# A decoder layer's MLP: a third seven-product unit in one column half, its weight sums made in the up stage, and the order of the returns and of the end

## The chip, the cores and the metric

The kernel runs on one core of one Trainium2 chip. Time is device microseconds (us) of that core, the median of several runs. The profile is one execution taken by the hardware profiler.

## The reference, cut to what matters

One decoder layer: a gated mix of sparse attention and retention, cross-attention, then an MLP, for 256 tokens of width 2048 in float32. The change touches only the MLP and the final norm (lines 1032 on). The MLP's hidden width is 8192.

```python
nm = rmsnorm(h, mlp_norm_w)
h = h + jnp.square(jax.nn.relu(nm @ w_up)) @ w_down
...
return rmsnorm(h, final_norm_w)
```

## The kernel before

**Engines.** PE (TensorE) multiplies, DVE (VectorE) and ACT (ScalarE) work on whole tiles, POOL (GpSimd) makes a power, SP starts loads. Each float32 operand is split into a high part of type fp32r (ACT copies it, L162) and a low part, the rest (DVE subtracts, L163). A product is then three matmuls: high x high, high x low, low x high. In the up stage the moving operand carries high and low tokens side by side: a high weight block takes one matmul of 512 columns, a low one a matmul of 256 (L158 is the helper that records every matmul).

**Pieces and units.** `mlp` cuts the hidden width into four pieces `p` of 2048 columns. A piece has an *up stage* of 16 units `Up(j, c)`: column block `j` (512 hidden columns, four PSUM banks), quarter `c` of the width 2048; 32 matmuls each. Below, up unit (3,0) is the first unit of the last block. Then comes a *down stage* of two halves `c` of the output columns (1024 each) with eight units `n` (256 hidden rows each). A *plain* unit (kind P, L1185) makes 8 products, 24 matmuls of 512 columns. A *seven-product* unit (kind S, L1170) makes 7 products, 21 matmuls, by Strassen and Winograd's scheme; it needs sums of weight blocks (`t1`, `t2`, made in `Down.prep`, L1134) and of activation blocks (`sums_up`, L1108). The string `KINDS` says which `n` are of kind S: 2 and 4 of eight, in both halves.

**PSUM.** Eight banks. Blocks `j` 0 and 2 use the two double tiles of pool `mm`, blocks 1 and 3 the other four banks. In a half, the double tiles `xa` (first 128 tokens) and `xb` (last 128) collect the plain products; the other four banks collect what is special to kind S (`m`). After the last S unit of a half, `combine` (L1197) makes two rows of sums from those banks, and `fold` (L1207) adds them to the result `hres`. `evac` (L1212) adds `xa` and `xb` to `hres` at the half's end. The next up stage begins in the double tiles that `evac` frees.

**Order.** The loop at the end of `mlp` (L1270 on) writes the order out: for each unit first the *next* unit's `prep` (load, high parts, low parts), then this unit's matmuls, then the `posts` that are due. A block's posts are `add_up` (adds the banks, right behind the block's last unit), `square_up` (relu, square, split; one unit later) and `sums_up` (two units later). Instructions go through `pin` (L153), which keeps each behind what was written before it on its own engine: DVE, ACT and SP run in that order. Loads take one of three `raw` buffers, high and low parts one of four buffers each.

**The end.** The last two units of the last piece are run as one pair (`plain` with two units): for each row block `i`, for each column half `j`, for each unit. `evac` then takes 1024 columns, `finish` (L1234) squares them on ACT (`scale`, L1225), multiplies with the final norm's weights on DVE, gets the power from POOL, scales four tiles of 512 columns (two on DVE, two on ACT) and starts the output transfers. `plain` also returns `scale` as a post at the end of each half of the last piece.

Of the kernel before, what the change touches and what calls it, by code (L numbers as in the profile page):

```python
# [9 lines left out]
F32 = mybir.dt.float32  # L10
F32R = mybir.dt.float32r
AF = mybir.ActivationFunctionType
ALU = mybir.AluOpType
# [4 lines left out]
P = 128  # L18
T = 256
D = 2048  # L20
EPS = 1e-6
# [44 lines left out]
class Kern:  # L66
# [86 lines left out]
    def pin(self, ins):  # L153
        if self.ordered:
            self.tc.keep_in_program_order(ins)
# [876 lines left out]
    def mlp(self):  # L1032
        nc, a = self.nc, self.a
        V, A, G, PE = nc.vector, nc.scalar, nc.gpsimd, nc.tensor
        pin = self.pin
        NP, KINDS = 4, "PPSPSPPP"
        hres = {}
        s8, r2 = self.keep("hs8", [2, 4]), self.keep("r2", [2])
        f8, ft = self.keep("fs", [2, 2]), self.keep("ft", [2])
        fw = []  # L1040
        tt = lambda o, x, y, op: pin(V.tensor_tensor(o, x, y, op=op))
        act = lambda o, x, f=AF.Copy, **kw: pin(A.activation(o, x, f, **kw))
# [7 lines left out]
        def hilo(n=1024):  # L1050
            return (self.st.tile([P, 1024], F32R, name=self.nm("hi"), tag="hi")[:, :n],
                    self.st.tile([P, 1024], F32R, name=self.nm("lo"), tag="lo")[:, :n])
# [12 lines left out]
        class Up:  # L1065
# [12 lines left out]

            def body(u):
                o = u.piece["banks"] = u.banks() if u.c == 0 else u.piece["banks"]  # L1080
                for k in range(4):
                    kt = u.c * 4 + k
                    x = self.h2hl[kt // 2][:, kt % 2, :]
                    for b in range(4):
                        s = slice(b * P, (b + 1) * P)
                        h, l = u.w[k]
                        self.mul(o[b], h[:, s], x, kt == 0, False)
                        self.mul(o[b][:, 0:T], l[:, s], x[:, 0:T], False, kt == 15)
                    if (u.p, u.j) == (0, 0) and k % 2 == 1:
                        back(u.c, k // 2)  # L1090
                return [self.add_up, self.square_up, self.sums_up] if u.c == 3 else []

        def add_up(u):
# [14 lines left out]
        def sums_up(u):  # L1108
            for k in range(2):
                n = 2 * u.j + k  # L1110
                if KINDS[n] != "S":
                    continue
                v = u.y[:, 2 * k:2 * k + 2, :].rearrange("p k (i t) -> p k i t", i=2)
                a11, a21, a12, a22 = v[:, 0, 0, :], v[:, 0, 1, :], v[:, 1, 0, :], v[:, 1, 1, :]
                s, sh, sl = self.w2("ss"), self.w2("sh", 512, F32R), self.w2("sl", 512, F32R)
                s1, s2, s3, s4 = (s[:, q * P:(q + 1) * P] for q in range(4))
                tt(s1, a21, a22, ALU.add)
                tt(s2, s1, a11, ALU.subtract)
                tt(s3, a21, a11, ALU.subtract)
                tt(s4, a12, s2, ALU.subtract)  # L1120
                self.split(sh, sl, s)
                u.piece["sums"][n] = [(sh[:, q * P:(q + 1) * P], sl[:, q * P:(q + 1) * P]) for q in range(4)]
# [5 lines left out]
        class Down:  # L1128
            def __init__(u, p, c, n, piece, group):
                u.p, u.c, u.n, u.piece, u.g = p, c, n, piece, group  # L1130
                u.kind = KINDS[n]
                u.last_s = n == max(k for k in range(8) if KINDS[k] == "S")

            def prep(u):  # L1134
                r0, c0 = u.p * 2048 + u.n * 256, u.c * 1024
                raw = load(a["w_down"][0][r0:r0 + 256, c0:c0 + 1024], 2)
                if u.kind == "P":
                    u.w = halves(raw)
                    return
                q = raw.rearrange("p (q n) -> p q n", q=4)  # L1140
                t1, t2 = self.big("t1", F32, (2, 512)), self.big("t2", F32, (2, 512))
                tt(t1, q[:, 1:2, :].to_broadcast([P, 2, 512]), q[:, 0::3, :], ALU.subtract)
                bh, bl = hilo()
                dh, dl = hilo(512)
                self.split(bh, bl, raw[:, 1024:])
                tt(t2[:, 0, :], q[:, 3, :], t1[:, 0, :], ALU.subtract)
                tt(t2[:, 1, :], q[:, 2, :], t2[:, 0, :], ALU.subtract)
                self.split(dh, dl, q[:, 0, :])
                (h1, l1), (h2, l2) = [[self.big(n, F32R, (2, 512)) for n in ("th", "tl")] for _ in range(2)]
                self.split(h1, l1, t1)  # L1150
                self.split(h2, l2, t2)
                u.w = {1: (dh, dl), 2: (bh[:, :512], bl[:, :512]), 3: (bh[:, 512:], bl[:, 512:]),
                       5: (h1[:, 0, :], l1[:, 0, :]), 7: (h1[:, 1, :], l1[:, 1, :]),
                       6: (h2[:, 0, :], l2[:, 0, :]), 4: (h2[:, 1, :], l2[:, 1, :])}

            def product(u, m, x, w, last):
                (xh, xl), (h, l) = x, w
# [12 lines left out]
            def body(u):  # L1170
                bank = u.g["bank"]
                if not bank:
                    ab, cd = u.g["rows"] = self.mmt("xa"), self.mmt("xb")
                    bank.update({2: ab[:, :512], 3: ab[:, 512:], 4: cd[:, :512], 8: cd[:, 512:]})
                if u.kind == "P":
                    return u.plain([u])
                if 1 not in bank:
                    bank.update({1: self.pst("m1"), 6: self.pst("m6"), 7: self.pst("m7"), 5: self.pot("m5")})
                s1, s2, s3, s4 = u.piece["sums"][u.n]
                x = {1: u.x(0, 0), 2: u.x(1, 0), 3: s4, 4: u.x(1, 1), 5: s1, 6: s2, 7: s3}  # L1180
                for m in (2, 3, 1, 5, 7, 6, 4):
                    u.product(m, x[m], u.w[m], u.last_s and m in (1, 5, 6, 7))
                return [combine, fold] if u.last_s else []

            def plain(u, us):  # L1185
                end = us[-1].n == 7
                for i in range(2):
                    for j in range(2):
                        for v in us:
                            for k in range(2):  # L1190
                                v.product((2, 3, 4, 8)[2 * i + j], v.x(k, i), v.w[2 * k + j], end and v is us[-1] and k == 1)
                    if end:
                        evac(us[-1], i)
                return [lambda u: scale(u.c)] if end and u.p == NP - 1 else []


        def combine(u):  # L1197
# [11 lines left out]
                o = hres[i, u.c]  # L1209
                stt(o, u.g["xy"][i], r2[:, i:i + 1], o, ALU.mult, ALU.add)  # L1210

        def evac(u, i):  # L1212
            o, c = hres[i, u.c], u.c
            stt(o, u.g["rows"][i], r2[:, i:i + 1], o, ALU.mult, ALU.add)
            if u.p < NP - 1:
                return
            if not fw:
                for k in range(2):
                    fw.append(self.big("fw", F32, (1024,)))
                    nc.scalar.dma_start(fw[k], a["final_norm_w"][k * 1024:(k + 1) * 1024].partition_broadcast(P))  # L1220
            if c == 1:
                finish(i)


        def scale(c, rows=range(2)):  # L1225
            for i in rows:
                o, v = hres[i, c], ft[:, i:i + 1]
                junk = self.big("junk", F32, (1024,))
                act(junk, o, AF.Square, accum_out=f8[:, i, c:c + 1])
                tt(o, o, fw[c], ALU.mult)  # L1230
                if c == 0:
                    pin(V.tensor_scalar(v, f8[:, i, 0:1], 1.0 / D, EPS, op0=ALU.mult, op1=ALU.add))

        def finish(i):  # L1234
            scale(1, [i])
            v = ft[:, i:i + 1]
            stt(v, f8[:, i, 1:2], 1.0 / D, v, ALU.mult, ALU.add)
            G.tensor_tensor(v, v, self.mhalf, op=ALU.pow)
            for k in range(4):
                o = hres[i, k // 2][:, (k % 2) * 512:(k % 2) * 512 + 512]  # L1240
                if k % 2:
                    act(o, o, scale=v)
                else:
                    pin(V.tensor_scalar(o, o, v, None, op0=ALU.mult))
                (nc.scalar if k % 2 else nc.sync).dma_start(self.out[0, i * P:(i + 1) * P, k * 512:(k + 1) * 512], o)
# [27 lines left out]
        while n < len(units):  # L1273
            u = units[n]
            two = n == len(units) - 2
            if n + 1 < len(units):
                units[n + 1].prep()
            self.ordered = True
            late = u.plain([u, units[n + 1]]) if two else u.body()
            posts += [[k, u, f] for k, f in enumerate(late)]  # L1280
            for t in list(posts):
                if t[0] == 0:
                    posts.remove(t)
                    t[2](t[1])
                else:
                    t[0] -= 1
            n += 2 if two else 1
# [29 lines left out]
```

## Time and profile before

| what | us |
|---|---|
| median of 3 runs | 1943.82 (1943.37 to 1943.91) |
| the profiled execution, its own time | 1943.98 |
| its span in the profile | 1942.2 |
| PE busy | 1916.1 (99%) |
| DVE busy | 1288.1 (66%) |
| ACT busy | 969.5 (50%) |

The span runs from the first to the last recorded event; the execution's own time is 1.8 us longer. Matmuls are pipelined and their ends are modelled, so what one costs PE in a stream is read as the distance from one start to the next. Idle time of an engine is put down to what released it.

### The profile page before, as it was taken

How to read it: one execution, taken by the hardware profiler on the slowest of the kernel's cores; microseconds unless marked ns; L12 is line 12 of the kernel's file. 1: busy time of each engine (PE TensorE's matmuls, PEld its weight loads, DVE VectorE, ACT ScalarE, POOL GpSimd, SP SyncE). 2: the span in 40 equal slices, each digit the busy share in tenths (PEclk: the TensorE clock that was granted, in tenths of full speed). 3: DMA queues.
4: the chain of work that ended last, by engine and by line, in shares of the span. 5: the costliest groups of instructions: out<-in, count | busy, mean ns of one | idle time of the engine just before them, and what ended most of it. 6: DMA issues, size and time to landing. Idle time of an engine off the chain costs nothing.

```text
span 1942.2 us, 26311 instructions
## 1 busy us (share of the span) xinstructions
PE 1916.1 (99%) x10534; PEld 1652.9 (85%) x10534; DVE 1288.1 (66%) x1553; ACT 969.5 (50%) x1308; POOL 85.4 (4%) x101
## 2 busy tenths in 40 slices
PE   8999999999999999999999999999999999999997
PEld 6888889888889999888889999888888888888885
DVE  6554577655766656887556756668757866875687
ACT  6444444455555554776444546544445434543554
POOL 1100021000000000321000000000000000000000
PEclk9999999999999999999999999999999999999999
DMA  8655545777877775333566654555655655665653
GB/s 267 211 177 195 182 168 171 238 239 247 282 242 242 251 247 193 130 125 114 195 220 220 211 176 151 165 189 188 195 182 186 211 180 178 198 201 185 193 195 130
DMA packets 173771, 382.17 MB, mean 197 GB/s; under 512 B 10592, under 2 KB 18784, under 8 KB 173648
## 3 DMA queue, kind: packets, MB, share of 16 engines
q1 hardware_dynamic: 169344, 373.96, 57.8%
q10 hardware_dynamic: 3504, 4.20, 0.7%
q0 software_dynamic: 800, 2.33, 0.4%
q8 instruction: 82, 1.34, 0.3%
q14 instruction: 41, 0.34, 0.1%
HBM read 374.17 MB, written 6.29 MB: 196 GB/s over the span
## 4 chain that ended last, share of the span: by engine, by line
PE 96%; DVE 2%; DMA 1%; issue 0%; ACT 0%; POOLq 0%; POOL 0%; SPq 0%; ACTq 0%; DVEq 0%
PE x L158 35%; PE u L158 18%; PE w L158 18%; PE xa L158 8%; PE xb L158 7%; PE acc L158 3%; PE m L158 2%; PE o L158 1%; PE s L158 1%; PE ro L158 1%; PE pT L816 1%; DVE lo L163 1%; DMA anw<-in_attn_norm_w_dram 0%; PE tr L287 0%; DVE hres L1043 0%
## 5 line engine op out<-in xcount | busy, mean ns | idle before, releaser
L163 DVE TENSOR_TENSOR lo<-raw,hi 128x1024 fp32r<-128x1024 f32 (+1 forms) x688 | 831.9, 1227 | 455.3 <-ACT hi L162 440.6
L162 ACT ACTIVATE hi<-raw 128x1024 fp32r<-128x1024 f32 (+1 forms) x688 | 704.6, 1047 | 688.1 <-PE x L158 336.2
L158 PE MATMUL u<-nhl,hi 128*128 128x512 f32 x1024 | 362.5, 398 | 3.5 <-DVE hres L1043 2.0
L158 PE MATMUL u<-nhl,lo 128*128 128x256 f32 x1024 | 288.0, 281 | 0.0
L158 PE MATMUL x<-hi,xh 128*128 128x512 f32 x704 | 283.0, 402 | 2.3 <-ACT hi L162 2.3
L158 PE MATMUL x<-hi,xl 128*128 128x512 f32 x704 | 278.3, 395 | 0.0
L158 PE MATMUL x<-lo,xh 128*128 128x512 f32 x704 | 277.5, 394 | 0.0
L158 PEld LDWEIGHTS u<-nhl,hi 128*128 128x128 f32 x1024 | 192.3, 188 | 50.9 <-DVE hres L1043 3.0
L158 PEld LDWEIGHTS u<-nhl,lo 128*128 128x128 f32 x1024 | 193.1, 189 | 0.1
L158 PEld LDWEIGHTS x<-lo,xh 128*128 128x128 f32 x704 | 133.2, 189 | 30.9 <-DVE lo L163 0.8
L158 PEld LDWEIGHTS x<-hi,xh 128*128 128x128 f32 x704 | 133.0, 189 | 30.3 <-ACT hi L162 2.7
L158 PEld LDWEIGHTS x<-hi,xl 128*128 128x128 f32 x704 | 133.1, 189 | 26.6
L158 PE MATMUL w<-xh,hi 128*128 128x256 f32 x512 | 145.2, 284 | 0.0
L158 PE MATMUL w<-xh,lo 128*128 128x256 f32 x512 | 144.2, 282 | 0.0
L158 PE MATMUL w<-xl,hi 128*128 128x256 f32 x512 | 144.1, 281 | 0.0
L158 PEld LDWEIGHTS w<-xh,hi 128*128 128x128 f32 x512 | 96.8, 189 | 1.4
L158 PEld LDWEIGHTS w<-xl,hi 128*128 128x128 f32 x512 | 96.8, 189 | 1.4
L158 PEld LDWEIGHTS w<-xh,lo 128*128 128x128 f32 x512 | 96.8, 189 | 0.0
L158 PE MATMUL w<-mh,hi 128*128 128x256 f32 x320 | 90.6, 283 | 0.0
L158 PE MATMUL w<-ml,hi 128*128 128x256 f32 x320 | 90.0, 281 | 0.0
L158 PE MATMUL w<-mh,lo 128*128 128x256 f32 x320 | 90.0, 281 | 0.0
L158 PE MATMUL xa<-lo,hh 128*128 128x512 f32 x208 | 81.8, 393 | 0.6 <-DVE lo L163 0.6
(310 smaller groups left out, 3016.6 us busy)
## 6 DMA issues: line engine op xcount, KB each, us to landing
raw<-in_w_in_dram SPq DMA_DIRECT2D x119, 1024.0 KB, 4.9
raw<-in_w_up_dram SPq DMA_DIRECT2D x64, 1024.0 KB, 5.4
raw<-in_w_down_dram SPq DMA_DIRECT2D x64, 1024.0 KB, 5.4
raw<-in_cmp_w_k_dram SPq DMA_DIRECT2D x16, 1024.0 KB, 4.9
raw<-in_w_b_dram SPq DMA_DIRECT2D x16, 1024.0 KB, 5.4
raw<-in_cmp_w_v_dram SPq DMA_DIRECT2D x16, 1024.0 KB, 5.0
raw<-in_w_a_dram SPq DMA_DIRECT2D x16, 1024.0 KB, 5.1
raw<-in_w_out_dram SPq DMA_DIRECT2D x16, 1024.0 KB, 5.1
```

The source lines that it names most:

```text
L158: self.pin(self.nc.tensor.matmul(out, l, r, start=start, stop=stop, skip_group_check=True))
L162: self.pin(self.nc.scalar.activation(hi, src, AF.Copy))
L163: self.pin(self.nc.vector.tensor_tensor(lo, src, hi.bitcast(F32), op=ALU.subtract))
L816: PE.transpose(pt[:, r * P:(r + 1) * P], sms[r // 2][:, r % 2, c:c + P], self.ident)
```

## The change

Half 0 of the output columns now takes kind S at `n` 1, 3 and 5, half 1 at 3 and 5. A block's activation sums are made if either half needs them. The weight sums of a down stage's first S unit are made behind up unit (3,0) (`ahead`), from a load of their own; the unit itself then only splits the blocks that enter as they are. The first up unit of pieces 1 to 3 does all four of its contraction steps for the first two banks, then for the other two. In the last pair the first row block goes unit by unit, the second column half by column half, and each half of 512 columns is evacuated, squared and multiplied by itself; in the last half `combine` and `fold` both stand right behind the last S unit. The final norm's weights are loaded where the first half is scaled, no longer where it is evacuated, and the second half is no longer scaled once more by a post. Three of the four last scalings run on DVE.

```diff
-        NP, KINDS = 4, "PPSPSPPP"
+        NP, KINDS = 4, ("PSPSPSPP", "PPPSPSPP")
...
@@ Up.body
+                late = u.p > 0 and (u.j, u.c) == (0, 0)
+                for bs in ((0, 1), (2, 3)) if late else (range(4),):
+                    for k in range(4):
...
+                        for b in bs:
...
@@ sums_up
-                if KINDS[n] != "S":
+                if "S" not in (KINDS[0][n], KINDS[1][n]):
...
@@ Down.prep
+                sums = None if u.early else u.sums(raw)
+                if sums:
+                    next(sums)
+                bh, bl = hilo()
+                dh, dl = hilo(512)
+                self.split(bh, bl, raw[:, 1024:])
+                if sums:
+                    next(sums)
+                self.split(dh, dl, raw[:, :512])
+                if sums:
+                    next(sums)
...
+            def sums(u, raw):
                 q = raw.rearrange("p (q n) -> p q n", q=4)
                 t1, t2 = self.big("t1", F32, (2, 512)), self.big("t2", F32, (2, 512))
                 tt(t1, q[:, 1:2, :].to_broadcast([P, 2, 512]), q[:, 0::3, :], ALU.subtract)
+                yield
                 tt(t2[:, 0, :], q[:, 3, :], t1[:, 0, :], ALU.subtract)
                 tt(t2[:, 1, :], q[:, 2, :], t2[:, 0, :], ALU.subtract)
+                yield
+                u.early = []
+                for t in (t1, t2):
+                    u.early.append([self.big(n, F32R, (2, 512)) for n in ("th", "tl")])
+                    self.split(*u.early[-1], t)
+                yield
+
+            def ahead(u):
+                r0, c0 = u.p * 2048 + u.n * 256, u.c * 1024
+                for _ in u.sums(load(a["w_down"][0][r0:r0 + 256, c0:c0 + 1024], 2)):
+                    pass
...
@@ Down.body
-                return [combine, fold] if u.last_s else []
+                return [lambda u: (combine(u), fold(u))] if (u.p, u.c) == (NP - 1, 1) else [combine, fold]
...
@@ plain
+                    order = [(v, j) for v in us for j in range(2)] if i == 0 else [(v, j) for j in range(2) for v in us]
+                    for v, j in order:
+                        for k in range(2):
+                            v.product((2, 3, 4, 8)[2 * i + j], v.x(k, i), v.w[2 * k + j], end and v is us[-1] and k == 1)
+                        if end and len(us) == 2 and v is us[-1]:
+                            evac(u, i, j)
+                    if end and len(us) == 1:
+                        evac(u, i)
+                return [scale] if end and u.p == NP - 1 and u.c == 0 else []
...
+        def evac(u, i, j=None):
+            c, p = u.c, u.p
+            v = slice(0, 1024) if j is None else slice(j * 512, j * 512 + 512)
+            o = hres[i, c][:, v]
+            stt(o, u.g["rows"][i][:, v], r2[:, i:i + 1], o, ALU.mult, ALU.add)
+            if j is not None:
+                square(i, c, v, 1 + j)
+                if j == 1:
+                    finish(i)
+
+        def square(i, c, v, n):
+            o = hres[i, c][:, v]
+            junk = self.big("junk", F32, (1024,))[:, v]
+            act(junk, o, AF.Square, accum_out=f8[:, i, n:n + 1])
+            tt(o, o, fw[c][:, v], ALU.mult)
+
+        def scale(u):
+            for k in range(2):
+                fw.append(self.big("fw", F32, (1024,)))
+                pin(nc.scalar.dma_start(fw[k], a["final_norm_w"][k * 1024:(k + 1) * 1024].partition_broadcast(P)))
+            for i in range(2):
+                square(i, 0, slice(0, 1024), 0)
+                pin(V.tensor_scalar(ft[:, i:i + 1], f8[:, i, 0:1], 1.0 / D, EPS, op0=ALU.mult, op1=ALU.add))
 
         def finish(i):
-            scale(1, [i])
             v = ft[:, i:i + 1]
-            stt(v, f8[:, i, 1:2], 1.0 / D, v, ALU.mult, ALU.add)
+            for n in (1, 2):
+                stt(v, f8[:, i, n:n + 1], 1.0 / D, v, ALU.mult, ALU.add)
...
-                if k % 2:
+                if k == 1:
                     act(o, o, scale=v)
...
@@ the loop
             posts += [[k, u, f] for k, f in enumerate(late)]
+            if isinstance(u, Up) and (u.j, u.c) == (3, 0):
+                next(d for d in units[n:] if isinstance(d, Down) and d.kind == "S").ahead()
```

## Rows read from the trace of the kernel before

**Rows 1.** Busy time by stretch, last piece: stretch, length, then PE to POOL, clock, DMA.
```profile
1752.30:1843.50 91.20, 90.51 (x514) 78.58 (x513) 54.74 (x63) 40.79 (x52) 0.00 (x0) 1.00 0.58 187
1843.50:1930.30 86.80, 86.15 (x372) 69.57 (x371) 72.67 (x78) 42.72 (x50) 0.55 (x1) 1.00 0.48 162
```
**Rows 2.** The chain that ended last: start, length, what; twelve matmuls of 512 columns.
```profile
1912.63 2.77 PE xa L158 x12
```
**Rows 3.** PE in order of time at piece 1's start: start, duration, instruction, [idle].
```profile
1398.66 0.28 PE L158 MATMUL u<-nhl,lo 128*128 128x256 f32 x1
1399.61 0.51 PE L158 MATMUL u<-nhl,hi 128*128 128x512 f32 x1 [0.68 <-DVE hres L1043]
```
**Rows 4.** DVE in order of time, last piece, up units (3,0) and (3,1).
```profile
1823.71 2.36 DVE L163 TENSOR_TENSOR lo<-raw,hi 128x1024 fp32r<-128x1024 f32 x2 [0.52 <-ACT hi L162]
1825.99 1.22 DVE L1043 SCALAR_TENSOR_TENSOR relu<-relu 128x1024 f32<-128x1024 f32 x1
...
1829.48 2.35 DVE L163 TENSOR_TENSOR lo<-raw,hi 128x1024 fp32r<-128x1024 f32 x2
```
**Rows 5.** ACT in order of time, the same units.
```profile
1827.24 1.06 ACT L162 ACTIVATE hh<-relu 128x1024 fp32r<-128x1024 f32 x1 [2.62 <-DVE relu L1043]
1828.20 2.00 ACT L162 ACTIVATE hi<-raw 128x1024 fp32r<-128x1024 f32 x2
```
**Rows 6.** PE in order of time, last piece, start of up unit (3,2).
```profile
1832.24 0.28 PE L158 MATMUL u<-nhl,lo 128*128 128x256 f32 x1
```
**Rows 7.** DVE in order of time: weights of a seven-product unit, last piece.
```profile
1850.65 1.22 DVE L1041 TENSOR_TENSOR t<-raw 128x1024 f32<-128x1024 f32 x1
1851.78 1.22 DVE L163 TENSOR_TENSOR lo<-raw,hi 128x1024 fp32r<-128x1024 f32 x1
1852.92 1.42 DVE L1041 TENSOR_TENSOR t<-raw,t 128x512 f32<-128x512 f32 x2
...
1854.85 2.35 DVE L163 TENSOR_TENSOR tl<-t,th 128x1024 fp32r<-128x1024 f32 x2
```
**Rows 8.** PE in order of time, last units: behind kind S, in the pair, last.
```profile
1912.47 0.39 PE L158 MATMUL xa<-hi,hh 128*128 128x512 f32 x1
...
1920.52 0.50 PE L158 MATMUL xa<-lo,hh 128*128 128x512 f32 x1 [0.48 <-DVE lo L163]
...
1930.08 0.39 PE L158 MATMUL xb<-lo,hh 128*128 128x512 f32 x1
```
**Rows 9.** DVE in order of time, last units and the end.
```profile
1912.05 0.69 DVE L1041 TENSOR_TENSOR u<-m,ux 128x512 f32<-128x512 f32 x1 [1.63 <-PE m L158]
...
1930.51 1.28 DVE L1043 SCALAR_TENSOR_TENSOR hres<-xb,r,hres 128x1024 f32<-128x1024 f32 x1 [0.20 <-PE xb L158]
1933.01 1.23 DVE L1041 TENSOR_TENSOR hres<-hres,fw 128x1024 f32<-128x1024 f32 x1 [1.22 <-ACT junk L1042]
...
1934.97 0.88 DVE L1244 TENSOR_SCALAR hres<-hres,ft 128x512 f32<-128x512 f32 x2 [0.67 <-POOL ft L1238]
...
1940.02 1.23 DVE L1041 TENSOR_TENSOR hres<-hres,fw 128x1024 f32<-128x1024 f32 x1 [0.36 <-DMA out_dram<-hres]
```
**Rows 10.** Groups by shape, ACT squares of 512 columns: busy us, mean ns, idle before.
```profile
L1042 ACT ACTIVATE junk<-hr 128x512 f32<-128x512 f32 x8 | 4.8, 599 | 14.0 <-DVE hres L1255 14.0
```
**Rows 11.** The chain that ended last: the last output transfer.
```profile
1936.87 3.03 DMA out_dram<-hres
```
**Rows 12.** The tile of the final norm's weights: transfers from issue to landing.
```profile
DMA to landing us min/median/max: 4.2/5.0/5.9
```
**Rows 13.** DVE in order of time, last piece: first use of those weights.
```profile
1887.62 1.22 DVE L1041 TENSOR_TENSOR hres<-hres,fw 128x1024 f32<-128x1024 f32 x1
```
**Rows 14.** PE in order of time at the kernel's start.
```profile
12.76 0.63 PE L158 MATMUL x<-hi,xl 128*128 128x512 f32 x1
13.19 0.63 PE L158 MATMUL x<-lo,xh 128*128 128x512 f32 x1
```
**Rows 15.** Busy time by stretch behind the last matmul; the clock is third from the end.
```profile
1935.00:1936.00 1.00, 0.00 (x0) 0.00 (x0) 0.86 (x2) 0.70 (x1) 0.00 (x0) 0.63 0.00 0
```

More of the change, by code (lines that the diff above doesn't have):

```diff
@@ L1035, in mlp @@
         pin = self.pin
-        NP, KINDS = 4, "PPSPSPPP"
+        NP, KINDS = 4, ("PSPSPSPP", "PPPSPSPP")
         hres = {}
         s8, r2 = self.keep("hs8", [2, 4]), self.keep("r2", [2])
-        f8, ft = self.keep("fs", [2, 2]), self.keep("ft", [2])
+        f8, ft = self.keep("fs", [2, 3]), self.keep("ft", [2])
         fw = []
@@ L1080, in body @@
                 o = u.piece["banks"] = u.banks() if u.c == 0 else u.piece["banks"]
[L1081 to L1090, printed above, removed]
+                late = u.p > 0 and (u.j, u.c) == (0, 0)
+                for bs in ((0, 1), (2, 3)) if late else (range(4),):
+                    for k in range(4):
+                        kt = u.c * 4 + k
+                        x = self.h2hl[kt // 2][:, kt % 2, :]
+                        for b in bs:
+                            s = slice(b * P, (b + 1) * P)
+                            h, l = u.w[k]
+                            self.mul(o[b], h[:, s], x, kt == 0, False)
+                            self.mul(o[b][:, 0:T], l[:, s], x[:, 0:T], False, kt == 15)
+                        if (u.p, u.j) == (0, 0) and k % 2 == 1:
+                            back(u.c, k // 2)
                 return [self.add_up, self.square_up, self.sums_up] if u.c == 3 else []
@@ L1114, in sums_up @@
                 a11, a21, a12, a22 = v[:, 0, 0, :], v[:, 0, 1, :], v[:, 1, 0, :], v[:, 1, 1, :]
-                s, sh, sl = self.w2("ss"), self.w2("sh", 512, F32R), self.w2("sl", 512, F32R)
+                s = self.w2("ss")
+                if len(u.piece["sums"]) < 2:
+                    sh, sl = self.w2("sh", 512, F32R), self.w2("sl", 512, F32R)
+                else:
+                    both = self.big("sb", F32R, (2, 512))
+                    sh, sl = both[:, 0, :], both[:, 1, :]
                 s1, s2, s3, s4 = (s[:, q * P:(q + 1) * P] for q in range(4))
@@ L1130, in __init__ @@
                 u.p, u.c, u.n, u.piece, u.g = p, c, n, piece, group
-                u.kind = KINDS[n]
-                u.last_s = n == max(k for k in range(8) if KINDS[k] == "S")
+                u.kind = KINDS[c][n]
+                u.last_s = n == KINDS[c].rindex("S")
+                u.early = None
             def prep(u):
@@ L1139, in prep @@
                     return
+                sums = None if u.early else u.sums(raw)
[9 more added lines that the diff above has]
+                    next(sums)
+                (h1, l1), (h2, l2) = u.early
+                u.w = {1: (dh, dl), 2: (bh[:, :512], bl[:, :512]), 3: (bh[:, 512:], bl[:, 512:]),
+                       5: (h1[:, 0, :], l1[:, 0, :]), 7: (h1[:, 1, :], l1[:, 1, :]),
+                       6: (h2[:, 0, :], l2[:, 0, :]), 4: (h2[:, 1, :], l2[:, 1, :])}
+            def sums(u, raw):
                 q = raw.rearrange("p (q n) -> p q n", q=4)
@@ L1142, in prep @@
                 tt(t1, q[:, 1:2, :].to_broadcast([P, 2, 512]), q[:, 0::3, :], ALU.subtract)
-                bh, bl = hilo()
-                dh, dl = hilo(512)
-                self.split(bh, bl, raw[:, 1024:])
+                yield
                 tt(t2[:, 0, :], q[:, 3, :], t1[:, 0, :], ALU.subtract)
                 tt(t2[:, 1, :], q[:, 2, :], t2[:, 0, :], ALU.subtract)
[L1148 to L1154, printed above, removed]
+                yield
[8 more added lines that the diff above has]
+                    pass
             def product(u, m, x, w, last):
@@ L1182, in body @@
                     u.product(m, x[m], u.w[m], u.last_s and m in (1, 5, 6, 7))
-                return [combine, fold] if u.last_s else []
+                if not u.last_s:
+                    return []
+                return [lambda u: (combine(u), fold(u))] if (u.p, u.c) == (NP - 1, 1) else [combine, fold]
             def plain(u, us):
@@ L1187, in plain @@
                 for i in range(2):
[L1188 to L1194, printed above, removed]
+                    order = [(v, j) for v in us for j in range(2)] if i == 0 else [(v, j) for j in range(2) for v in us]
[7 more added lines that the diff above has]
+                return [scale] if end and u.p == NP - 1 and u.c == 0 else []
         def combine(u):
@@ L1210, in fold @@
                 stt(o, u.g["xy"][i], r2[:, i:i + 1], o, ALU.mult, ALU.add)
[L1212 to L1232, printed above, removed]
+        def evac(u, i, j=None):
[19 more added lines that the diff above has]
+                pin(V.tensor_scalar(ft[:, i:i + 1], f8[:, i, 0:1], 1.0 / D, EPS, op0=ALU.mult, op1=ALU.add))
         def finish(i):
-            scale(1, [i])
             v = ft[:, i:i + 1]
-            stt(v, f8[:, i, 1:2], 1.0 / D, v, ALU.mult, ALU.add)
+            for n in (1, 2):
+                stt(v, f8[:, i, n:n + 1], 1.0 / D, v, ALU.mult, ALU.add)
             G.tensor_tensor(v, v, self.mhalf, op=ALU.pow)
```

## The prediction

> **What bounds the kernel now.** I read the view that splits the span by stages first, because the change touches only the MLP at the end. In its last piece the tensor engine (PE) is busy for 90.5 of the 91.2 us of the up stage and 86.2 of the 86.8 us of the down stage, while VectorE (DVE) has 54.7 and 72.7 [rows 1]. The reader should see two things: the time is PE's instruction stream, so removed matmuls count in full; and DVE is a mean of 60% busy in the up stage, which says nothing yet about one particular place in it. So I then read the instructions in order of time on PE, DVE and ACT around each place that the diff touches. DVE, ACT and SP execute the MLP in the order in which the program writes it (`pin`), so a step put between two others delays everything behind it on that engine.
>
> **Fewer matmuls.** A plain unit has 24 matmuls of 512 columns, a seven-product unit 21. Twelve of them take 2.77 us start to start [rows 2], 0.231 us each. One more seven-product unit per piece in four pieces removes 4 x 3 = 12 matmuls, all on PE's path: **-2.8 us**. The second half keeps two such units, at later places; its matmul count is unchanged.
>
> **The return to the up stage.** At the start of pieces 1 to 3 PE issues four matmuls into the banks freed first and then waits for DVE to evacuate the others: 1398.66 to 1399.61 where 0.12 would do, and the first matmul after the wait takes 0.51 instead of 0.40 us [rows 3]. That is 0.83 to 0.93 us, three times. The new order gives the freed banks 16 of 32 matmuls, half of a unit of about 5.6 us (a sixteenth of the stage of rows 1), so 2.8 us of cover against the 1.6 us that the wait ends after the unit's start: **-2.6 us**. What has to be ready earlier are the unit's second weights, prepared one unit ahead.
>
> **Sums made ahead.** This is the largest term. After up unit (3,0) the program now makes the weight sums of the first seven-product unit: one subtraction of 1024 columns, two of 512, two splits of 1024. DVE needs 1.22 + 1.42 + 2.35 = 4.99 us for them [rows 7]; consecutive DVE instructions overlap by some 0.09 us (1850.65 to 1851.78 for one of 1.22), and the second low part waits 0.1 us for ACT, so DVE is held for 4.8 us. Where do they stand? Behind the low parts of unit (3,1) and ahead of the squaring of column block 2, and so ahead of the low parts of unit (3,2) [rows 4]. Today, in the last piece, those parts begin at 1829.48; the first is done 1.22 us later, at 1830.70. PE's first matmul that reads one is the second of unit (3,2), at 1832.24 [rows 6], 63 matmuls before the stage's end at 1843.4. The cover is 1.54 us, and 4.8 are added. ACT runs in order too: the high parts of unit (3,2) stand right behind the squared block's split, which waits for DVE [rows 5], and move from 1828.20 to 1833.0, their end to 1834.1. PE would thus issue its first matmul at 1834.1 and its second at 1835.5, 3.3 us late; with a restart as in rows 3, 3.4 us. The second pair of parts is needed half a unit later and is there. Up unit (3,3) has the third activation sums ahead of it, but starts 3.3 us later too, and I find its parts ready by 0.5 us or more. The pattern is the same in four pieces: 4 x 3.4 = **+13.6 us**. Bounds: 2.6 us each, if ACT and DVE overlap better than the rows show, to 3.7 with a second restart. The four extra weight loads are hidden: they are issued from SP a slot earlier than used, and no DVE row in rows 4 waits for a DMA.
>
> What the step buys: without it the new second unit would have its 6.9 us of DVE work (1.22 + 1.22 + 1.42 + 0.69 for the short split + 2.35) right behind the banks' additions, where the down stage has little room. With it the third seven-product unit adds 6.9 - 2.35 = 4.5 us to DVE's down stage and 4.7 are moved away, so its 72.7 of 86.8 us stays [rows 1]. Following the units in order I find every part of the first half ready 0.7 us or more ahead of PE: 0, with an upper bound of 0.5 us per piece. The additional activation sums after block 0 stand as those of blocks 1 and 2 do today, which delay nothing.
>
> **The final norm's weights** are now loaded behind ACT's high parts for the second half's first unit, about 4 us ahead of the half's end. The load took 4.2 to 5.9 us [rows 12], and its first reader runs at 1887.62 [rows 13], 1.6 us behind the half's last matmul. It can be late by 0.7 us, about the slack of the weights queued behind it: 0, bound +0.7.
>
> **The last two units.** From the first matmul behind the last seven-product unit to the last matmul are 24 + 47 = 71 steps, 16.4 us at 0.231; the rows say 1912.47 to 1930.08, 17.6, so 1.2 us of waits, the largest at 1920.52 [rows 8]. Now that unit is followed at once by the joint pair. DVE's combination begins 0.42 us before its end (1912.05 against 1912.47) [rows 8, 9], and combination (four of 0.69 less their overlap, 2.5), both folds (two of 1.28, 2.4) and the first low part (1.22) come in that order: ready 5.7 us into the pair. The pair reads it with its 15th matmul, at 3.2 us: 2.5 late, and 0.4 more for the second part and restarts. About 3.0 in place of 1.2: **+1.8 us**.
>
> **The end.** Today DVE evacuates 1024 columns at 1930.51, multiplies at 1933.01 behind ACT's squares, and scales at 1934.97, 4.89 us after the last matmul's start [rows 8, 9]. In halves, one round is 0.69 for an evacuation as of 512 columns in rows 9, 0.6 for the squares [rows 10], 0.1 to 0.2 for their read-out and 0.6 for the product: 2.05. This would give 3.4 us, but DVE has four such rounds in a row with the first rows' finish between them (0.8 to the power's return, as from 1934.24 to 1934.97 today, and 1.3 for three scalings of 0.44): 0.43 + 8.2 + 2.1 + 0.8 = 11.5 us from the last matmul of the first quarter, while PE needs 30 x 0.231 = 7.0 from there. So the scaling starts 4.6 us after the last matmul: -0.3. The last output leaves 1.36 instead of 1.90 us after that (1936.87, rows 11): -0.5. Finally the old kernel squares and multiplies the second half once more behind its outputs: the last DVE instruction starts at 1940.02 and takes 1.23 us, though the last output is out at 1936.87 + 3.03 = 1939.90 [rows 9, 11]. That goes: -1.35. Together **-2.1 us**, so the pair and the end give -0.3. Bounds for both: -2.5 to +1.
>
> **Sum.** -2.8 - 2.6 + 13.6 - 0.3 = +7.9 us on the profiled execution's 1943.98 us (span 1942.2), that is 1951.9; this execution lies 0.16 us over the median of 1943.82, so I forecast 1951.7 us. About 0.2%, 3.9 us, is what a measurement of this kernel can tell from no change.
>
> **Rivals.**
> (1) *Faster:* the 4.8 us at up unit (3,0) are absorbed. It decides by whether the high and low parts of unit (3,2) get past the sums. For it: DVE idles for 36 us of the up stage [rows 1]. Against it: rows 4 and 5 show ACT idle in front of the squared block with later copies queued. If all is hidden, 1951.7 - 13.6 = 1938.1 us.
> (2) *The clock:* four gaps of 3.4 us, with one matmul inside, could lower PE's clock. At the kernel's start 512 columns are issued 0.43 us apart [rows 14], against 0.23 later, which are the levels 1.2 and 2.4 GHz. After the last matmul at 1930.08 the granted clock stayed at 1.00 for some 5 us and fell between 1935 and 1936 [rows 15], which speaks against a fall here. If each gap cost one up unit at half speed, 5.6 us, it would be 1951.7 + 22 = 1974 us. The Trainium skill ("TensorE: Matmul & The Clock Gate", section "Why this matters for your kernels") warns that idle gaps between bursts of matmuls send the clock back to half; by that rule the time would be this one, and the row on the end bears it out only for a longer gap.
> (3) *The third unit starves:* DVE, near its limit in the first half, is late there by 1.3 us more per piece: 1951.7 + 5 = 1957 us. Against it: the 4.7 us moved away match the 4.5 added.
>
> **How the numbers follow.** Forecast 0.82, rival 1 0.08, rival 2 0.04, rival 3 0.06. The forecast's own bounds are 1943.8 + (4 x 2.6 - 5.4 - 2.5) = 1946.3 and 1943.8 + (4 x 3.7 - 5.4 + 1 + 2.7) = 1956.9 at worst; 1947 to 1956 holds 8 in 10, leaving out rivals 1 and 2. Slower by over 0.2% begins at 1947.7: most of the forecast, rivals 2 and 3, 0.86. Within 0.2%: sums half absorbed, 0.05. Faster: rival 1 and a little, 0.09.
>
> **What would show it.** Right: in each piece PE waits for DVE's low part (and ACT's high part) at the start of up unit (3,2), 3 us in all, with the subtractions of the weight sums just before on DVE; no wait on the evacuation at the returns; 12 matmuls of 512 columns fewer; a wait of 2 to 3 us in the last pair; nothing on DVE behind the last output. Wrong: up unit (3,2) starting without a gap, a granted clock below 1.00 behind it, or waits in the first half of the down stage.

## The result and the profile after

The changed kernel takes 1962.36 us (median of four runs, 1960.52 to 1963.09) against 1943.8: a ratio of 1.0094, 95% interval 1.0081 to 1.0106. The profiled execution took 1962.1 us with a span of 1960.3, 18.1 over the old one. The direction was forecast, the size not: 7.9 us were expected, and the time lies beyond the range of 1947 to 1956.

The waits of PE in the MLP, by what ended them (us in total, times, longest); a wait of 0.8 us at the MLP's start, which the old kernel has too, is left out:

```profile
PE u L158 <- ACT hi L162: 8.2, 4, 2.1
PE u L158 <- DVE lo L163: 3.6, 4, 1.0
PE xa L158 <- DVE lo L163: 2.4, 1, 2.4
PE xb L158 <- DVE hres L1043: 1.7, 1, 1.7
PE xa L158 <- DVE hres L1043: 0.8, 1, 0.8
```

The first two lines are the forecast waits in front of up unit (3,2), once in each piece. The third is the forecast wait in the last pair. The last two were not forecast. The wait for an evacuation at the returns is gone [rows 3].

PE in order of time around up unit (3,2) of the first piece:

```profile
1300.12 0.28 PE L158 MATMUL u<-nhl,lo 128*128 128x256 f32 x1
1302.45 0.70 PE L158 MATMUL u<-nhl,hi 128*128 128x512 f32 x1 [2.06 <-ACT hi L162]
1303.90 0.58 PE L158 MATMUL u<-nhl,lo 128*128 128x256 f32 x1 [0.75 <-DVE lo L163]
1304.28 0.63 PE L158 MATMUL u<-nhl,hi 128*128 128x512 f32 x1
1304.71 0.41 PE L158 MATMUL u<-nhl,lo 128*128 128x256 f32 x1
1304.92 0.63 PE L158 MATMUL u<-nhl,hi 128*128 128x512 f32 x1
```

The unit's second matmul was due at 1300.47 (0.12 and 0.23 behind the first row) and starts at 1303.90, 3.43 us late. Then look at the distances: a pair of matmuls takes 0.64 us (1304.28 to 1304.92), where it takes 0.35 at full clock (1299.77 to 1300.12 in the same trace). DVE in order of time shows what stood in front:

```profile
1294.20 1.22 DVE L1041 TENSOR_TENSOR t<-raw 128x1024 f32<-128x1024 f32 x1
1295.46 1.42 DVE L1041 TENSOR_TENSOR t<-raw,t 128x512 f32<-128x512 f32 x2
1296.79 2.43 DVE L163 TENSOR_TENSOR tl<-t,th 128x1024 fp32r<-128x1024 f32 x2
1299.15 1.22 DVE L1043 SCALAR_TENSOR_TENSOR relu<-relu 128x1024 f32<-128x1024 f32 x1
...
1302.63 2.35 DVE L163 TENSOR_TENSOR lo<-raw,hi 128x1024 fp32r<-128x1024 f32 x2
```

From the first subtraction to the squaring DVE is held for 4.95 us; the old kernel went straight to the squaring [rows 4]. Busy time by stretch, for the first piece and (second fence) the third; the granted clock is the third number from the end:

```profile
1301.00:1303.00 2.00, 0.55 (x1) 0.20 (x1) 1.51 (x2) 2.00 (x3) 0.00 (x0) 0.89 0.27 111
1303.00:1305.00 2.00, 1.25 (x5) 1.00 (x5) 2.00 (x3) 0.35 (x1) 0.00 (x0) 0.50 0.02 8
1305.00:1306.00 1.00, 1.00 (x5) 0.81 (x5) 0.88 (x4) 0.05 (x1) 0.00 (x0) 0.50 0.00 0
```
```profile
1664.00:1666.00 2.00, 0.50 (x1) 0.19 (x1) 2.00 (x3) 1.47 (x2) 0.00 (x0) 1.00 0.07 29
1666.00:1668.00 2.00, 1.98 (x12) 1.76 (x13) 1.97 (x5) 0.00 (x0) 0.00 (x0) 1.00 0.00 0
```

In the first piece the clock fell to 0.50 (1.2 GHz) inside the wait and was back at 1309.4, after 5.5 us of matmuls at that level; in the third, behind the same wait, it stayed at 1.00. The chain that ended last prices it. It has the same 63 matmuls behind the wait in each piece:

```profile
1303.90 13.65 PE u L158 x63
...
1485.62 12.71 PE u L158 x63
...
1666.02 11.14 PE u L158 x63
...
1844.76 12.86 PE u L158 x63
```

At full clock 63 matmuls of this mix take 11.1 us, as in the third line. The others are longer by 2.5, 1.6 and 1.7 us, 5.8 together (5.9 in the expectations below, which took 11.1). The last pair, PE in order of time:

```profile
1934.44 0.40 PE L158 MATMUL xa<-hi,hl 128*128 128x512 f32 x1
1937.20 0.59 PE L158 MATMUL xa<-lo,hh 128*128 128x512 f32 x1 [2.35 <-DVE lo L163]
...
1939.98 0.80 PE L158 MATMUL xa<-hi,hh 128*128 128x512 f32 x1 [0.85 <-DVE hres L1043]
1940.57 0.63 PE L158 MATMUL xa<-hi,hl 128*128 128x512 f32 x1
...
1948.09 0.50 PE L158 MATMUL xb<-hi,hh 128*128 128x512 f32 x1 [1.71 <-DVE hres L1043]
...
1950.76 0.40 PE L158 MATMUL xb<-lo,hh 128*128 128x512 f32 x1
```

The pair begins at 1931.44 and its last matmul starts at 1950.76: 19.3 us, where 47 steps of 0.231 take 10.9. Of the 8.5 us of excess (1.2 in the old kernel, there with the unit ahead of the pair), 2.5 are the low part, 3.0 the two waits for an evacuation, and most of the rest the clock, low again from 1937.5 to 1944.3. DVE behind the last matmul:

```profile
1951.19 0.75 DVE L1043 SCALAR_TENSOR_TENSOR hres<-xb,r,hres 128x512 f32<-128x512 f32 x1 [1.68 <-PE xb L158]
...
1954.35 1.28 DVE L1284 TENSOR_SCALAR hres<-hres,ft 128x512 f32<-128x512 f32 x3 [0.67 <-POOL ft L1278]
```

DVE waited for PE here, and the scaling starts 3.6 us after the last matmul (1950.76 to 1954.35).

### The profile page after: what moved, and what is told of

It is laid out like the page before. It is cut to its first block, busy times and chain, and to the rows that moved or that the text cites. A ratio compares the mean times of both kernels' runs of the same rounds, so it can differ in the third digit from the quotient of the medians.

```text
span 1960.3 us, 26355 instructions
## 1 busy us (share of the span) xinstructions
PE 1922.4 (98%) x10522; PEld 1656.2 (84%) x10522; DVE 1310.2 (67%) x1599; ACT 974.1 (50%) x1318; POOL 85.3 (4%) x101
## 4 chain that ended last, share of the span: by engine, by line
PE 93%; DVE 4%; issue 1%; ACT 1%; DMA 1%; POOLq 0%; POOL 0%; DVEq 0%; SPq 0%; ACTq 0%
PE x L158 34%; PE w L158 17%; PE u L158 16%; PE xa L158 8%; PE xb L158 7%; PE acc L158 3%; PE m L158 3%; PE o L158 1%; DVE lo L163 1%; PE s L158 1%; PE ro L158 1%; DVE t L1041 1%; PE pT L816 1%; DVE tl L163 0%; ACT hi L162 0%
## 5 line engine op out<-in xcount | busy, mean ns | idle before, releaser
L158 PE MATMUL u<-nhl,hi 128*128 128x512 f32 x1024 | 367.6, 402 | 9.7 <-ACT hi L162 8.2
```

Source lines behind the costliest of these rows:

```text
L158: self.pin(self.nc.tensor.matmul(out, l, r, start=start, stop=stop, skip_group_check=True))
```

## The experiments

All times are medians; ratios are against runs of the kernel before in the same session. The first four keep the changed kernel and touch only the sums.

**The sums behind up unit (3,2).**

```diff
-            if isinstance(u, Up) and (u.j, u.c) == (3, 0):
+            if isinstance(u, Up) and (u.j, u.c) == (3, 2):
                 next(d for d in units[n:] if isinstance(d, Down) and d.kind == "S").ahead()
```

> The weight sums are made behind up unit (3,2) instead of (3,0); all else as changed. Theory A (the place: they stand in front of unit (3,2)'s weights with 1.5 us of cover, which costs 3.4 us of waiting in each of four pieces, and the clock falls behind three of the four waits, 5.9 us): no wait in the up stage, granted clock 1.00 there, 1962.4 - 13.7 - 5.9 = 1942.8 us, 1941 to 1945. Rival B (the work is too much wherever it stands: DVE then makes PE wait at the start of the down stage instead): a wait of 2 us or more in front of the first or second down unit in each piece, 1951 us or more.

1943.5 us, ratio 0.9999 (0.9990 to 1.0009). PE has no wait from the first up unit's start to the last pair (the 0.8 us missing in the first line below stand at the MLP's start, in the old kernel too), and in the up stage and the down stage of the first piece it is busy throughout at full clock, though DVE has 62.2 us of work in the first stretch, where the old kernel has 57.0:

```profile
1220.00:1312.00 92.00, 91.20 (x530) 79.66 (x528) 62.19 (x81) 47.21 (x71) 0.00 (x0) 1.00 0.55 182
1312.00:1397.00 85.00, 85.00 (x367) 68.81 (x367) 70.33 (x74) 40.69 (x44) 0.00 (x0) 1.00 0.61 201
```

The place costs 18.9 us (1962.36 against 1943.5). Rival B falls: the same work two units later is free.

**No sums ahead.** The two lines of the loop that call `ahead` are left out.

> No sums ahead: the first seven-product unit of each piece makes its own in its preparation, and the four extra loads go. Theory A: no wait in the up stage; by the DVE rows the third down unit's low part is ready some 1.2 us late in each piece, too short a wait for the clock: 1942.8 + 4.8 = 1947.6 us, 1943 to 1950. Rival B (the sums have to be made ahead, this unit starves without): waits of 3 us and more per piece in the first half of the down stage, 1955 us or more.

1950.29 us, ratio 1.0034 (1.0021 to 1.0047): 6.8 us over the run above instead of 4.8, just above the range. PE waits for the low part of the third down unit in each piece, as expected, but it loses 1.7 us per piece: the second low part is late too, ACT's high part ahead of them comes some 0.3 us late, and the first matmul behind each wait is slower:

```profile
1323.32 0.50 PE L158 MATMUL xa<-lo,hh 128*128 128x512 f32 x1 [0.71 <-DVE lo L163]
1324.46 0.50 PE L158 MATMUL xa<-lo,hh 128*128 128x512 f32 x1 [0.18 <-DVE lo L163]
```

So making the sums ahead is worth 6.8 us where it is covered, and loses 12 us (1962.36 against 1950.29) where it was put.

**The wait filled.** Nine matmuls that nothing reads run inside the wait:

```diff
+            if isinstance(u, Up) and (u.j, u.c) == (3, 2):
+                fill, x = self.mmt("fill"), self.h2hl[0][:, 0, :]
+                for _ in range(9):
+                    self.mul(fill[:, :512], x[:, :P], x, True, True)
```

> As changed, but nine matmuls of 512 columns into a bank that nothing reads stand in front of up unit (3,2), 2.1 us of PE work inside the first part of the wait (2.06 us by the trace). Theory A, its second part (the idle time lowers the clock): the waits stay 3.4 us long from the end of unit (3,1), but the granted clock stays at 1.00 behind them; 1962.4 - 5.9 = 1956.5 us, 1955 to 1958. Rival C (the slow matmuls behind the wait come from something else, such as DVE and ACT catching up on the same memory): matmuls of 512 columns still 0.43 us apart behind the wait, 1961 us or more.

1956.61 us, ratio 1.0068 (1.0051 to 1.0085), 5.75 below the changed kernel. Unit (3,2) comes as late as before, and the clock stays at 1.00 in all four pieces:

```profile
1299.76 2.24 PE L158 MATMUL fill<-nhl 128*128 128x512 f32 x9
1301.98 0.50 PE L158 MATMUL u<-nhl,hi 128*128 128x512 f32 x1
1303.43 0.39 PE L158 MATMUL u<-nhl,lo 128*128 128x256 f32 x1 [0.94 <-DVE lo L163]
1303.65 0.40 PE L158 MATMUL u<-nhl,hi 128*128 128x512 f32 x1
```

The work that DVE and ACT do behind the wait is unchanged, so rival C falls: idle time of PE lowered the clock. Of the 18.9 us, 13.1 are waiting (1956.61 against 1943.5) and 5.75 the clock; the trace of the changed kernel has 4 x 3.43 = 13.7 and 5.8.

**Half of the sums.** Behind (3,0) the generator is advanced twice (the subtractions), behind (3,2) once more (the splits).

> Behind up unit (3,0) only the three subtractions (2.6 us of DVE), the two splits behind unit (3,2). Theory A: the cover of 1.5 us takes most of it, a wait of 1.1 to 1.3 us per piece is left and the clock stays at 1.00: 1942.8 + 4.8 = 1947.6 us, 1946 to 1949. Rival B: waits of the down stage as well, 1951 or more.

1947.3 us, ratio 1.0019 (1.0010 to 1.0029), in the middle of the range. Four waits of 0.9 us are left, 3.7 in all, and the granted clock is 1.00 behind each (second fence: the first piece):

```profile
PE u L158 <- DVE lo L163: 3.7, 4, 0.9
```
```profile
1299.00:1306.00 7.00, 6.08 (x35) 5.06 (x34) 6.01 (x10) 4.40 (x6) 0.00 (x0) 1.00 0.67 226
```

The wait follows the cover: 2.6 us of work less 1.5 of cover.

The next four start from the sums behind up unit (3,2), 1943.5 us.

**The last unit's weights first.**

```diff
-            if n + 1 < len(units):
+            if n + 1 < len(units) and not two:
                 units[n + 1].prep()
...
+            if n == len(units) - 3:
+                units[n + 2].prep()
             for t in list(posts):
```

> From here on the base is the changed kernel with the sums behind up unit (3,2), 1943.5 us. In this run the last unit's weights are prepared ahead of the combination and the folds of the last seven-product unit. Theory D (two causes at the end: the low parts queued behind combination and folds, 2.7 us and the clock behind it 1.6; and each half's evacuation, which holds PE out of the other half of the same double tile, 0.8 and 2.4): the first goes, the second stays or grows by up to 1 us because DVE still has the folds to do: 1938.5 to 1941. Rival E (only the DVE chain of half evacuations sets the end): the last matmul comes earlier but the end by less than 1 us, 1942.5 or more.

1940.72 us, ratio 0.9984 (0.9975 to 0.9994). The wait for the low part is gone. Of the two waits for evacuations, 0.8 and 2.4 us in the run that this one starts from, the first grows to 1.5:

```profile
PE xb L158 <- DVE hres L1043: 2.4, 1, 2.4
PE xa L158 <- DVE hres L1043: 1.5, 1, 1.5
```

**Evacuations behind the row block.** `evac(u, i, 0)` and `evac(u, i, 1)` move from inside the loop to its end.

> Base, but in the last pair both halves of a row block are evacuated behind the block's last matmul, in the same rounds. Theory D: PE waits no longer for an evacuation (0.8 and 2.4 us gone), the wait for the low part stays 2.4; two rounds instead of one lie behind the last matmul, +2 us: 1941 to 1942.5. Rival E: the chain on DVE is as long as before, 1943 to 1944.

1942.63 us, ratio 0.9994 (0.9985 to 1.0003). PE no longer waits for an evacuation; the low part's 2.4 us stay. That PE's waits go fits theory D; the time lies between the ranges of D and E and decides nothing alone.

**The old return order.** `late = False`.

> Base, but the first up unit of pieces 1 to 3 again runs its four banks in turn. If the return's new order is worth what the rows of before say, three waits of 0.83 us and a restart each come back: +2.6 us, 1946.1 (1945.5 to 1946.7). If the evacuation has moved or the waits are hidden otherwise: 1943.5.

1946.29 us, ratio 1.0014 (1.0005 to 1.0023): +2.8 us. The return's order is worth what the rows gave, 2.6.

**Both repairs of the end.** The weights first as above, and:

```diff
-                        if end and len(us) == 2 and v is us[-1]:
-                            evac(u, i, j)
...
+                    if end and len(us) == 2:
+                        vs = [slice(j * 512, j * 512 + 512) for j in range(2)]
+                        for v in vs:
+                            o = hres[i, 1][:, v]
+                            stt(o, u.g["rows"][i][:, v], r2[:, i:i + 1], o, ALU.mult, ALU.add)
+                        for j in range(2):
+                            square(i, 1, vs[j], 1 + j)
+                        finish(i)
```

> Base with the last unit's weights prepared ahead of combination and folds, and with each row block's two halves evacuated behind its last matmul, the second evacuation ahead of the first product, so that rounds overlap. Theory D: no wait over 0.5 us in the pair, clock 1.00 to the end, last matmul 8 us earlier than in the base and some 1 us more behind it: 1935.5 to 1938. Rival E: 1940 or more.

1935.86 us, ratio 0.9961 (0.9947 to 0.9976): 0.4% faster than the kernel before. PE has no wait from the start of the piece to its last matmul. DVE in order of time, behind that matmul (its start is 1924.46):

```profile
1924.90 1.41 DVE L1043 SCALAR_TENSOR_TENSOR hres<-xb,r,hres 128x512 f32<-128x512 f32 x2 [0.48 <-PE xb L158]
1926.44 1.35 DVE L1041 TENSOR_TENSOR hres<-hres,fw 128x512 f32<-128x512 f32 x2
1927.70 0.34 DVE L1043 SCALAR_TENSOR_TENSOR ft<-fs,ft 128x1 f32<-128x1 f32 x2
1928.71 1.28 DVE L1290 TENSOR_SCALAR hres<-hres,ft 128x512 f32<-128x512 f32 x3 [0.67 <-POOL ft L1284]
```

The second evacuation covers the first squares, so the scaling starts 4.25 us after the last matmul, 4.89 before the change [rows 8, 9].

The last four close the account.

**Two seven-product units in both halves**, from the kernel just above: `KINDS = ("PPPSPSPP", "PPPSPSPP")`.

> The kernel of b4_both, 1935.9 us, but with two seven-product units in both halves (3 and 5), none at 1; their sums still made behind up unit (3,2) for unit 3. Theory A (the third unit is worth its 12 matmuls, PE has no wait in the down stage with it): +2.8, 1938.7 (1938 to 1939.5). Rival F (its DVE work costs hidden waits that go with it): 1936 to 1937.5.

1939.17 us, ratio 0.9975 (0.9966 to 0.9985); by the ratios the third unit gives 0.0014 of 1943.8, 2.7 us. The intervals of the two ratios overlap, so the size rests on the traces: PE's four down stages are together 2.7 us longer here, and PE has no wait in either kernel. The third unit's DVE work costs PE nothing.

**The old place with the repaired end:** `(3, 0)` again.

> The kernel of b4_both with the sums back behind up unit (3,0): the parts add up if the four waits and the clock behind them cost the same as before: 1935.9 + 18.9 = 1954.8 us, 1953 to 1956.5; the clock falls in some of the four pieces and not in others. If a part of the 18.9 belonged to the old end: 1951 or less.

1954.22 us, ratio 1.0051 (1.0035 to 1.0068): +18.4. The place costs the same with either end. Here the fourth piece is the one whose clock stayed at 1.00:

```profile
1300.00:1312.00 12.00, 9.15 (x35) 7.61 (x36) 8.67 (x11) 6.91 (x8) 0.00 (x0) 0.72 0.46 149
1480.00:1500.00 20.00, 16.98 (x84) 14.20 (x84) 13.60 (x19) 10.38 (x14) 0.00 (x0) 0.91 0.63 211
1660.00:1680.00 20.00, 17.28 (x82) 14.27 (x81) 13.40 (x18) 9.43 (x13) 0.00 (x0) 0.83 0.64 213
1838.00:1860.00 22.00, 19.00 (x105) 16.06 (x104) 17.03 (x23) 12.51 (x16) 0.00 (x0) 1.00 0.69 237
```

**Single banks for the last half**, from the weights-first kernel with its evacuations inside the row block:

```diff
+                    if (u.p, u.c) == (NP - 1, 1):
+                        bank.update({m: self.pst("xs") for m in (2, 3, 4)})
+                        bank[8] = self.pot("xs")
...
+                if 1 not in bank and (u.p, u.c) == (NP - 1, 1):
+                    ab, cd = self.mmt("ma"), self.mmt("mb")
+                    bank.update({1: ab[:, :512], 6: ab[:, 512:], 7: cd[:, :512], 5: cd[:, 512:]})
...
+            src = u.g["rows"][i] if j is None else u.g["bank"][(2, 3, 4, 8)[2 * i + j]]
+            stt(o, src, r2[:, i:i + 1], o, ALU.mult, ALU.add)
```

> The kernel of b1_prep_first, 1940.7 us, whose halves are evacuated in the middle of a row block, but in the last half the four plain products lie in four single-bank tiles and the special ones in the double tiles. Theory G (PE waits for the evacuation because both halves lie in one tile): no wait of PE on an evacuation, 1935.5 to 1937.5. Rival H (a bank that DVE reads holds PE out of another bank too): the waits of 1.5 and 2.4 us stay, 1940 or more.

1937.77 us, ratio 0.9969 (0.9957 to 0.9980), 3 us below the same kernel with double tiles and 0.3 above the range. PE has no wait left from the first return on. So theory G holds: PE waited because the two halves lie in one tile, not because DVE was reading another bank. The last matmul starts at 1924.22, and DVE's rounds, one behind the other, set the end:

```profile
1918.35 0.74 DVE L1043 SCALAR_TENSOR_TENSOR hres<-xs,r,hres 128x512 f32<-128x512 f32 x1
...
1930.14 1.28 DVE L1292 TENSOR_SCALAR hres<-hres,ft 128x512 f32<-128x512 f32 x3 [0.67 <-POOL ft L1286]
```

**The old kernel without its second scaling.** Left out is work whose result nothing reads.

> The kernel before, without the second scaling of the second half behind its outputs (work whose result nothing reads). If the span ends with the last output then: the profiled span 1.35 us shorter, 1940.85, and 1942.4 us (1941.5 to 1943.2). If something else ends the execution: no change.

1943.54 us, ratio 0.9997 (0.9988 to 1.0007): no difference that can be measured. From the start of the last evacuation to the end of the span it is 11.1 us (1930.88 to 1942.0) against 11.7 before (1930.51 to 1942.2), so 0.6 us at most, not 1.35.

## Why the prediction was wrong

Two terms failed, each enough to carry the time beyond the range: the clock, put at nothing, cost 5.8 us, and the pair and the end, put at -0.3 and at most +1, came to +4.7. With both put right, 1951.7 + 5.8 + 5.0 gives 1962.5 us, against 1962.36 measured.

- **The sums' place: right in place and size.** Forecast were four waits of 3.4 us at up unit (3,2), first for ACT's high part, then for DVE's low part; the trace has 3.43. The rule that carried it, cover of 1.54 us against 4.8 of added work in an engine that runs in order, also gave the halved version, 1.1 us by the rule and 0.9 measured.
- **The clock: the step that failed.** "Rival 2" got 0.04, and the main sum held the clock at 1.00 through four gaps. It fell at three of four: 5.8 us by the chain, 5.75 by the run with the wait filled. The argument against it rested on one event, the clock's stay at 1.00 for 5 us after the last matmul [rows 15]. One event could not carry it: the same wait lowers the clock in one piece and not in another, and which piece is spared changed between two kernels. The price was wrong as well, 5.6 us per gap where 1.6 to 2.5 were found: the clock fell inside the gap or up to 1.3 us behind it and was back after 3.3 to 5.5 us of matmuls at the low level. The Trainium skill ("TensorE: Matmul & The Clock Gate", section "Why this matters for your kernels") asks to avoid long idle gaps between bursts of matmuls, because the clock returns to half. The trace agrees in three of the four gaps of 3.4 us (0.50 behind them) and not in the third piece (1.00); behind the four of 0.9 us it is 1.00.
- **The last pair: the second step that failed, a wait missed.** "+1.8 us" priced only the low parts behind combination and folds; those came 2.5 us late as forecast. Missed was that a half's evacuation holds PE out of the other half of its tile: 0.8 and 1.7 us; and behind the wait for the low part the clock fell once more. The excess of the pair is 8.5 us instead of 3.0. The Trainium skill ("PSUM — Partial Sum Buffer", section "PSUM bank collisions raise a hardware error") says that the hardware does not stall an engine whose access to a bank collides with another engine's, and that accesses of two engines to different banks run clean. The single-bank run agrees: it keeps the order and loses the waits, so the wait came with the double tile, from the program.
- **The end: "-2.1 us" was about right, its parts not.** From the last matmul's start to the span's end it is 9.5 us (1950.76 to 1960.3) against 12.1 [rows 8], -2.6. The duplicate scaling gave 0.6 at most, not 1.35: its last instruction was the last on DVE, but the span's end hardly moved without it. The scaling's start gave 1.3 instead of 0.3 (3.6 us after the last matmul, 4.89 before): PE was so late that DVE waited for it, and the chain of four rounds did not set the end. Where nothing else held that chain, in the single-bank run, it took 11.8 us (1918.35 to 1930.14), against 11.1 by the prediction (11.5 less the 0.43 ahead of the first evacuation).
- **Right:** -2.8 for twelve matmuls (2.7 by the traces), -2.6 for the returns (2.8), nothing for the third unit on DVE. Nothing was lost on the norm's weights, as forecast, but with little to spare: they took 6.8 to 7.8 us to land instead of 4.2 to 5.9, and were issued 7.0 us ahead of their first reader.

The account of the changed kernel's span: -2.8 - 2.6 + 13.7 (waits) + 5.8 (clock) + 7.3 (pair, 8.5 - 1.2) - 2.6 (end) = +18.8, against 18.1 measured; the 0.7 us between them are not placed.

## What to carry to other kernels

A mean load says little about a step put between two others on an engine that runs in order: find the next instruction that PE needs from that engine, take its cover, and compare it with the step's duration. Moved two units on, the same 4.8 us were free. A wait of PE of 2 to 3 us should be priced with the clock behind it, even where one gap in the trace left the clock alone; and where a half-finished tile is evacuated, look whether PE still writes the rest of the same tile.

## What was not expected of the hardware

The same gap of 3.4 us with one matmul inside lowered the granted clock in three of four pieces, and the third or the fourth piece was spared, depending on the kernel. With the last unit's weights first, two gaps of 1.5 and 2.4 us in the last pair went ahead of a fall: the clock is at 0.71 in the two microseconds behind the end of the second, at 1925.08.

```profile
1915.00:1925.00 10.00, 6.23 (x26) 4.43 (x24) 7.45 (x13) 2.17 (x5) 0.55 (x1) 1.00 0.06 20
1925.00:1927.00 2.00, 1.93 (x6) 1.58 (x7) 0.71 (x2) 0.72 (x2) 0.00 (x0) 0.71 1.05 366
```

A gap of 2.4 us does not always do it: with the sums behind (3,2) the second wait of 2.4 us in the pair left the clock at 1.00. Why one piece is spared stays open; no run here separates it.
